# A hybrid decoder block on one core: plain fp32 for one small layer, and a new order around the output projection

## The chip, the cores and the metric

The kernel runs on one core of a Trainium2 chip. The metric is device time in microseconds (us), from the first to the last instruction of one execution and what lies around it, as the median of three runs. The engines are named as in the profile: PE is TensorE (its weight load is PEld), DVE is VectorE, ACT is ScalarE, POOL is GpSimd, SP is SyncE, which here only issues transfers.

## The reference, cut to what matters

One decoder layer on 256 tokens of width 1024: attention by two groups of heads, then a feed-forward layer that picks experts out of 16,384 (PEER). What the change touches is the compressed branch (a small two-layer network over blocks of 32 tokens), the six modulation vectors that come from the condition `c`, and the output projection.

```python
cond = jax.nn.silu(c)
mod = (cond @ ada_w[l] + ada_b[l]).reshape(c.shape[0], 6, 1, D_MODEL)
sh_a, sc_a, g_a, sh_f, sc_f, g_f = (mod[:, i] for i in range(6))
h = rmsnorm(x, norm1_g[l]) * (1 + sc_a) + sh_a
x = x + g_a * nsa_diff_mixer(h, w_in[l], w_out[l], ...)     # mixed @ w_out at its end
h = rmsnorm(x, norm2_g[l]) * (1 + sc_f) + sh_f
x = x + g_f * peer_ffn(h, peer_wq[l], peer_sub_keys[l], peer_u[l], peer_v[l])

def compress_blocks(tok, pos_enc, w1, w2, starts):          # called for keys and for values
    idx = starts[:, None] + np.arange(CMP_BLOCK)[None, :]
    blocks = tok[:, idx] + pos_enc[None, None, :, None, :].astype(tok.dtype)
    ...
    return jax.nn.gelu(flat @ w1) @ w2                      # w1: 2048 x 256
```

In the differential heads `o_d` is normed (a square root of a mean of squares) before it joins the mixed row.

## The kernel before, in words

**Stages.** Up to 64 us the input projection runs for the first 16 chunks of 128 columns (`k_load`, `k_prep`, `k_mm`, lines 211 to 242). From there to about 145 us come the attention heads, the compressed branch and the rest of the input projection, then the tail of the heads and the output projection (to 184 us), four early chunks of the expert layer's query product (L743), the second norm, and from 202 us the expert layer: 128 tiles of `peer_u` (products L89 to L91 for the name `up`), the choice of experts, and 128 tiles of `peer_v`.

**Products in three parts.** A weight tile of 128 x 1024 is loaded into one of 5 `raw` buffers by SP (`load`, L67), ACT casts it to a high part `w_hi` (L73), DVE subtracts to get `w_lo` (L74), and `mm3` (L88) multiplies high by high (L89) and the two mixed terms (L90, L91). So each such tile costs one ACT and one DVE instruction, and three products for one. In two places plain fp32 products of one pass of the code are used instead, without a split: L743 and L865, both for the expert layer's queries.

**The compressed branch.** `evac_ctok` (L308) adds the position code to the token columns in PSUM, writes the sum to a buffer and splits it into `e_sb` (high) and `cd` (low); `cmp_gen` (L380) takes 8 tiles of `cmp_w1`, 4 for keys and 4 for values, splits each, and issues 4 x 3 products of 256 columns with 30 stationary columns. Then come a Gelu (L391), two transposes (L395) and the small second layer.

**The order of the work** between 64 and 184 us is written out by hand: each word of `ORDER` advances one generator by one step, and the compiler's scheduler then places the instructions on the engines, near that order. The words: `cmp` the compressed branch; `nA`, `nB` the rest of the input projection; `ds0` to `ds3` and `do0`, `do1` the differential heads' logits and outputs; `pgt`, `ogt` and `ct` logits, outputs and the compressed part of the other heads (group g, half t); `w0` to `w3` the output projection with the first half (kh=0) of its inputs, which are the NSA heads' rows. Its second half (kh=1), fed by the differential heads, follows after `ORDER` in a loop of its own (`w_out_part(dp, 1, ...)`, L706).

**The late modulation sums.** 24 of the 40 column tiles of `ada_w` are summed late (`more_ada`, L192): SP loads 512 KB into one of 4 `adal` buffers, DVE multiplies by `cond` and sums (L151). `ada` does that at its place, `adf` only after the last marked instruction. What is left over after `ORDER` is summed there. The sums are needed for the residual (`mod` at L711) and for the second norm, so after the second half of the output projection's first tile.

**Differential heads' output** (`diff_out`, L587): transposes (L595), copies by ACT (`dpt`, L597), products with the values (L603), squares with sums by ACT (L609), a square root by ACT (L610, needs the table of square roots), reciprocal and product by DVE (L611, L612: `od`), transposes, and a split into `mixed` (L620 by ACT, L621 by DVE). kh=1 of the output projection needs `mixed` from both `do1` and `do0`.

**Second norm and queries.** After the projection PE sums squares (L704), ACT takes the root (L733), DVE the reciprocal (L734); then DVE and ACT make the normed rows (L756 to L759), and `bq`, `qe` (L764 to L766) empty the early query products' banks. The same banks hold the first `up` tiles.

Of the kernel before, what the change touches and what calls it, by code (L numbers as in the profile page):

```python
# [13 lines left out]
F32 = mybir.dt.float32  # L14
F32R = mybir.dt.float32r
# [4 lines left out]
AF = mybir.ActivationFunctionType  # L20
# [4 lines left out]
P = 128  # L25
D = 1024
# [9 lines left out]
nB cmp p01 cmp p00 cmp c0 p11 o01 o01 nB p11 adf o01 ada ada p00 c0 ada ada p00 o01 p11 p11 p00 o00  # L36
o00 adf p11 p11 p11 p10 adf p11 p10 p11 p11 o11 p10 p10 p10 o01 adf p10 ds3 o11 adf o01 p10 ds3 p10
ds3 p10 o11 p10 p10 o11 adf ds3 ds2 ds3 ds2 ds2 ds3 o10 ds2 ds2 o00 ada ada o00 o10 adf do1 o10 o10
o11 ada adf adf adf do1 ds2 adf o11 adf do0 do1 w0 do0 do0 do1 w0 w1 do1 w2 ada do0 w2 do0 w1 w3 ada
w3 ada  # L40
""".split()
KD = 8
T = 256
# [14 lines left out]
def block_kernel(ctx: ExitStack, tc: tile.TileContext, I, out):  # L58
    nc = tc.nc
    V, S, G, PE = nc.vector, nc.scalar, nc.gpsimd, nc.tensor  # L60
# [6 lines left out]
    def load(src, n=D, pool=None, name="raw", **kw):  # L67
        t = (pool or raw_pool).tile([P, D], F32, name=name, **kw)
        nc.sync.dma_start(t[:, :n], src)
        return t  # L70

    def split(src, hi, lo, eng=None):
        S.copy(hi, src)  # L73
        return (eng or V).tensor_sub(lo, src, hi.bitcast(F32))  # L74

    def split_tile(t, n=D, eng=None):
        hi = hl_pool.tile([P, D], F32R, name="w_hi")
        lo = hl_pool.tile([P, D], F32R, name="w_lo")
        split(t[:, :n], hi[:, :n], lo[:, :n], eng)
        return hi, lo  # L80

    def load_split(src, n=D, eng=None, first=False):
        if first:
            with tc.high_priority(offset=None if first is True else first):
                return split_tile(load(src, n), n, eng)
        return split_tile(load(src, n), n, eng)

    def mm3(ps, w, m, start, stop):  # L88
        PE.matmul(ps, w[0], m[0], start=start, stop=False)  # L89
        PE.matmul(ps, w[0], m[1], start=False, stop=False)  # L90
        PE.matmul(ps, w[1], m[0], start=False, stop=stop)  # L91
# [23 lines left out]
    sm = ph1.enter_context(tc.tile_pool(name="sm", bufs=4))  # L115
# [5 lines left out]
    def bank(tag):  # L121
        return (pst if tag == "tr" else psp).tile([P, 512], F32, name=tag)
# [3 lines left out]
    eps_t = one.tile([P, 1], F32, name="eps_t")  # L126
# [13 lines left out]
    w2 = cmpc[:, 32:544].rearrange("p (a b c) -> p a b c", a=2, b=2)  # L140
# [9 lines left out]
    def ada_sum(ct, w):  # L150
        return V.tensor_tensor_reduce(out=w, in0=w, in1=cond, scale=D / 2, scalar=0.0,  # L151
                               op0=ALU.mult, op1=ALU.add, accum_out=mod[:, ct:ct + 1])
# [39 lines left out]
    def more_ada(fence=False):  # L192
        ct = next(pend_ada, None)
        if ct is None:
            return
        w = wk.tile([P, D], F32, name="adal", bufs=4)
        nc.sync.dma_start(w, I["ada_w"][ct])
        if fence and mark:
            with tc.issue_after(mark[-1].ins):
                ada_sum(ct, w)  # L200
        else:
            ada_sum(ct, w)
# [73 lines left out]
    wk = wk_stack.enter_context(tc.tile_pool(name="wk", bufs=2))  # L276
# [8 lines left out]
    def projN(name, n, per, evac):  # L285
# [14 lines left out]
        for t in range(2):  # L300
# [1 line left out]
        yield  # L302


    ctok = [[wk.tile([P, 512], F32R, name=n, bufs=b).rearrange("p (o b) -> p o b", o=16)
             for n, b in (("e_sb", 8), ("cd", 2))] for kv in range(2)]

    def evac_ctok(kv):  # L308
        def f(ps):
            full = wk.tile([P, 512], F32, name="lg_sb", bufs=3).rearrange("p (o b) -> p o b", o=16)  # L310
            for g in range(2):
                src = ps[g * 64:(g + 1) * 64].rearrange("p (b o) -> p o b", o=16)
                for half in range(2):
                    pr = slice(64 * half, 64 * half + 64)
                    V.tensor_add(full[pr, :, g * 15:(g + 1) * 15], src[:, :, half:half + 15],
                                 pos[pr, kv, :, None].to_broadcast([64, 16, 15]))
            hi, lo = [x[:, :, 0:30] for x in ctok[kv]]
            return split(full[:, :, 0:30], hi, lo)
        return f


# [58 lines left out]
    def cmp_gen():  # L380
        for kv in range(2):
            hps = bank("tr")
            for l in range(4):
                hi, lo = load_split(I["cmp_w1"][kv, l], D)
                for o in range(4):
                    c = slice(o * 256, (o + 1) * 256)
                    mm3(hps[:30, 0:256], [x[:, l * 4 + o, 0:30] for x in ctok[kv]], (hi[:, c], lo[:, c]),
                        l == 0 and o == 0, l == 3 and o == 3)
                yield
            hd = wk.tile([P, T], F32, name="on", bufs=1)  # L390
            S.activation(hd[:30], hps[:30, 0:256], AF.Gelu_apprx_tanh)  # L391
            yield
            tp = bank("tr")
            for hh in range(2):
                PE.transpose(tp[:, hh * 32:hh * 32 + 30], hd[:30, hh * P:(hh + 1) * P], ident[:30, :30])  # L395
            V.tensor_copy(hidT[kv][:, :, 0:30], tp[:, 0:64].rearrange("p (a b) -> p a b", a=2)[:, :, 0:30])
            yield
            if kv == 0:
                ps = bank("tr")
                for hh in range(2):  # L400
                    PE.matmul(ps[:, 0:30], w2[:, 0, hh], hidT[0][:, hh, 0:30], start=hh == 0, stop=hh == 1)
                for x in KC:
                    S.copy(x.rearrange("p g c -> p (g c)"), pcz[0][:, 0, 0:32])
                for g in range(2):
                    pr = slice(64 * g, 64 * g + 64)
                    split(ps[pr, g * 15:g * 15 + 15], KC[0][pr, g, 0:15], KC[1][pr, g, 0:15])
                done.add("KC")
            else:
                ps = bank("tr")
                for g in range(2):  # L410
                    for hh in range(2):
                        PE.matmul(ps[0:15, g * 64:g * 64 + 64], hidT[1][:, hh, g * 15:g * 15 + 15],
                                  w2[:, 1, hh, 0:64], start=hh == 0, stop=hh == 1)
                for g in range(2):
                    for h in range(4):
                        S.copy(vbd[g][32 * h:32 * h + 15, 64 * h:64 * h + 64], ps[0:15, g * 64:g * 64 + 64])
                done.add("vbd")
            yield
# [236 lines left out]
    def item(n):  # L655
        if n[:2] == "ds":
            return diff_soft(int(n[2]))
        if n[:2] == "do":
            return diff_out(int(n[2]))
        if n == "nA":  # L660
            return projN("w_inA", 280, 3, evacA)
        if n == "nB":
            return projN("w_inB", 512, 2, evacB)
        if n == "cmp":
            return cmp_gen()
        h = int(n[1])
        if n[0] == "c":
            return nsa_c(h)
        if n[0] == "p":
            return nsa_p(h, int(n[2]))  # L670
        if n[0] == "o":
            return nsa_o(h, int(n[2]))
        if n[0] == "w":
            return w_out_part(h, 0, WO[h])
        raise ValueError(n)

    items = {}
    for n in ORDER:
        if n in ("ada", "adf"):
            more_ada(n == "adf")  # L680
        else:
            if n not in items:
                items[n] = item(n)
            next(items[n], None)
# [53 lines left out]
    for i, tag in enumerate(("o", "tr", "mm", "mm")):  # L738
        with tc.high_priority(offset=None):
            w = load(I["peer_wq"][i])  # L740
# [539 lines left out]
```

## Time and profile before

| | |
|---|---|
| time, median of 3 runs | 971.66 us (971.08 to 974.53) |
| the profiled execution | 968.78 us, of which its span 967.0 us |
| PE busy, DVE busy, ACT busy | 927.8, 765.9, 496.2 us |
| mean granted TensorE clock | 0.990 |
| data moved | 197.55 MB, 204 GB/s over the span |

The span is what the trace shows, from the first to the last instruction; the time has some 1.8 us more around it. A busy time sums an engine's instructions; since matrix products are pipelined and their ends are modelled, a stretch in which PE counts as fully busy can still be one in which it runs at half clock. The clock stands in the windows as a share of 2.4 GHz: 1.00 and 0.50 are its two levels, and values between them are stretches that hold both.

### The profile page before, as it was taken

Reading aid. Unit: us, or ns where it says so; the run is one execution under the profiler, and the core shown is the slowest. Engines: PE = TensorE matmul, PEld = TensorE weight load, DVE = VectorE, ACT = ScalarE, POOL = GpSimd, SP = SyncE. Lnnn points to the kernel's source line nnn. Section 1 sums busy time; section 2 is a strip of 40 time slices with the busy share of each in tenths; the row PEclk is TensorE's granted clock in tenths of the full one; section 3 lists DMA queues with packets and bytes.
Section 4 is the critical chain, followed back from the end, with each engine's and each line's share of the span. In section 5 each row is a group of like instructions: output and inputs, shape, how many; then the busy total and the mean of one; then the engine's idle time right before and its main releaser. Section 6 shows DMA issues by size and latency. Waiting matters only on the chain.

```text
span 967.0 us, 18674 instructions
## 1 busy us (share of the span) xinstructions
PE 927.8 (96%) x7118; PEld 681.8 (71%) x7118; DVE 765.9 (79%) x2033; ACT 496.2 (51%) x901; POOL 14.5 (2%) x27
## 2 busy tenths in 40 slices
PE   5989997999999999999999999999999998999995
PEld 3987877888888888899999998444544543554442
DVE  7978888788475799468988988799999988655664
ACT  4458874574333465554444445545444544555552
POOL 0000010000000000000000000000000000000001
PEclk9999998999999999999999999999999999999998
DMA  9978557686544356755555555655555669756631
GB/s 361 357 296 267 156 176 239 236 293 190 181 156 155 123 176 200 234 195 184 177 189 181 178 192 177 217 198 181 191 193 182 214 218 331 233 177 198 212 112 48
DMA packets 54132, 197.55 MB, mean 204 GB/s; under 512 B 6145, under 2 KB 6417, under 8 KB 53522
## 3 DMA queue, kind: packets, MB, share of 16 engines
q1 hardware_dynamic: 52706, 191.38, 59.2%
q0 software_dynamic: 608, 3.17, 1.0%
q10 hardware_dynamic: 720, 1.74, 0.5%
q8 instruction: 57, 0.93, 0.4%
q14 instruction: 41, 0.34, 0.1%
HBM read 193.11 MB, written 3.15 MB: 203 GB/s over the span
## 4 chain that ended last, share of the span: by engine, by line
PE 85%; DVE 6%; DMA 4%; ACT 3%; issue 2%; SPq 0%; DVEq 0%; ACTq 0%
PE y L1077 28%; PE up L89 11%; PE up L90 11%; PE up L91 11%; PE up L865 4%; PE gps L988 3%; DMA raw<-in_ada_w_dram 2%; PE lg L350 2%; PE mm L90 1%; PE mm L91 1%; PE mm L89 1%; PE o L524 1%; DMA raw<-in_w_inK_dram 1%; PE gps L873 1%; DVE w_hi L794 1%
## 5 line engine op out<-in xcount | busy, mean ns | idle before, releaser
L1077 PEld LDWEIGHTS <-wt 128*128 128x128 f16 x1500 | 144.0, 98 | 170.3 <-DVE wt L794 5.1
L793 ACT ACTIVATE w_lo<-raw 128x1024 f16<-128x1024 f32 x128 | 135.2, 1057 | 173.7 <-PE y L1077 84.3
L793 ACT ACTIVATE w_hi<-raw 128x1024 f16<-128x1024 f32 x128 | 135.2, 1056 | 170.2 <-PE up L91 85.8
L794 DVE SCALAR_TENSOR_TENSOR w_lo<-raw,w_lo 128x1024 f16<-128x1024 f32 x128 | 156.3, 1221 | 62.9 <-ACT w_lo L793 60.5
L794 DVE SCALAR_TENSOR_TENSOR w_hi<-raw,w_hi 128x1024 f16<-128x1024 f32 x128 | 156.1, 1219 | 54.9 <-ACT w_hi L793 54.6
L1077 PE MATMUL y<-w_hi,wt 128*128 128x512 f16 x756 | 174.0, 379 | 2.0 <-DVE wt L794 2.0
L1077 PE MATMUL y<-w_lo,wt 128*128 128x512 f16 x744 | 171.0, 379 | 0.5 <-DVE wt L794 0.4
L89 PE MATMUL up<-h,w_hi 128*128 128x256 f16 x512 | 139.6, 273 | 2.1 <-ACT bq L765 2.1
L91 PE MATMUL up<-h,w_hi 128*128 128x256 f16 x512 | 139.6, 273 | 0.0
L90 PE MATMUL up<-h,w_hi 128*128 128x256 f16 x512 | 139.6, 273 | 0.0
L89 PE MATMUL up<-h,w_lo 128*128 128x256 f16 x504 | 137.4, 273 | 0.0
L91 PE MATMUL up<-h,w_lo 128*128 128x256 f16 x504 | 137.4, 273 | 0.0
L90 PE MATMUL up<-h,w_lo 128*128 128x256 f16 x504 | 137.4, 273 | 0.0
L794 DVE SCALAR_TENSOR_TENSOR wt<-st,wt 128x256 f16<-128x256 f32 x128 | 53.6, 419 | 4.7 <-ACT wt L793 4.7
L90 PEld LDWEIGHTS <-w_hi 128*128 128x128 f16 x512 | 50.1, 98 | 8.2 <-issue 2.3
L793 ACT ACTIVATE wt<-st 128x256 f16<-128x256 f32 x128 | 51.3, 401 | 7.6 <-PE y L1077 5.6
L90 PEld LDWEIGHTS <-w_lo 128*128 128x128 f16 x512 | 50.1, 98 | 6.1
L91 PEld LDWEIGHTS <-w_hi 128*128 128x128 f16 x512 | 50.1, 98 | 5.8
L91 PEld LDWEIGHTS <-w_lo 128*128 128x128 f16 x512 | 50.0, 98 | 5.8
L89 PEld LDWEIGHTS <-w_lo 128*128 128x128 f16 x512 | 50.1, 98 | 5.7
L89 PEld LDWEIGHTS <-w_hi 128*128 128x128 f16 x512 | 50.2, 98 | 5.5
L972 DVE TENSOR_TENSOR B<-iota,kT 128x576 f16<-128x576 f16 (+1 forms) x64 | 27.1, 424 | 28.9 <-PE gps L988 28.8
(366 smaller groups left out, 1489.2 us busy)
## 6 DMA issues: line engine op xcount, KB each, us to landing
raw<-in_peer_u_dram SPq DMA_DIRECT2D x128, 512.0 KB, 3.5
raw<-in_peer_v_dram SPq DMA_DIRECT2D x128, 512.0 KB, 3.8
adal<-in_ada_w_dram SPq DMA_DIRECT2D x24, 512.0 KB, 4.5
adaw<-in_ada_w_dram SPq DMA_DIRECT2D x16, 512.0 KB, 5.5
raw<-in_w_inK_dram SPq DMA_DIRECT2D x16, 512.0 KB, 7.4
wraw<-in_peer_wq_dram SPq DMA_DIRECT2D x12, 512.0 KB, 4.3
raw<-in_cmp_w_dram SPq DMA_DIRECT2D x8, 512.0 KB, 4.4
raw<-in_w_out_dram SPq DMA_DIRECT2D x8, 512.0 KB, 4.4
```

Of the source, the lines that this page charges most:

```text
L89: PE.matmul(ps, w[0], m[0], start=start, stop=False)
L90: PE.matmul(ps, w[0], m[1], start=False, stop=False)
L91: PE.matmul(ps, w[1], m[0], start=False, stop=stop)
L350: PE.matmul(out, q[x][pr, ts], rhs, start=i == 0, stop=i == 2)
L524: PE.matmul(o[:, h * 64:(h + 1) * 64], pt[:, h * P:(h + 1) * P], vst[sb][:, b, g], start=False, stop=bi == len(blocks) - 1 and h == 3)
L793: S.activation(hi, src, AF.Copy, scale=scale, **kw)
L794: V.scalar_tensor_tensor(lo, src, scale, hi, ALU.mult, ALU.subtract, accum_out=chk[:, i:i + 1])
L865: PE.matmul(ps, w[:, k * P:(k + 1) * P], h2[:, k], start=k == 0, stop=k == KD - 1)
L873: PE.matmul(sps[:, t], qs[p][:, t * P:(t + 1) * P], sk[:, p], start=True, stop=True)
L972: V.tensor_tensor(pairs(x), io, kT[:, i, t0:t0 + NT, None, :].to_broadcast(four), ALU.is_equal)
L988: PE.matmul(ps[:, q, 0:n], A[:, q], Bg[i][:, q], start=i == 0, stop=i == 1)
L1077: PE.matmul(yps[t][n], w[:, ts], m[:, ns], start=j == 0 and first, stop=j == NJ - 1 and last)
```

## The change

It has three parts. First, the compressed branch's first layer takes the unsplit token columns and the unsplit weight tile: 16 plain fp32 products for each of keys and values in the place of 48, with no ACT cast, no DVE subtraction, and the `raw` buffer held until the products are done. Second, the last lines of `ORDER` are rewritten: the modulation sums that stood between `o00`, `do1` and `o11` stand among and after `w0` to `w3`. Third, a word `sqrt` issues a square root of one column, ahead of `do0`.

```diff
-o11 ada adf adf adf do1 ds2 adf o11 adf do0 do1 w0 do0 do0 do1 w0 w1 do1 w2 ada do0 w2 do0 w1 w3 ada
-w3 ada
+o11 ada adf do1 ds2 o11 sqrt do0 do1 w0 do0 do0 do1 w0 adf w1 do1 adf w2 adf do0 w2 do0 w1 adf w3 adf ada
+w3 ada ada
...
-    ctok = [[wk.tile([P, 512], F32R, name=n, bufs=b).rearrange("p (o b) -> p o b", o=16)
-             for n, b in (("e_sb", 8), ("cd", 2))] for kv in range(2)]
+    ctok = [wk.tile([P, 512], F32, name="e_sb", bufs=8).rearrange("p (o b) -> p o b", o=16) for kv in range(2)]
...
-                    V.tensor_add(full[pr, :, g * 15:(g + 1) * 15], src[:, :, half:half + 15],
+                    r = V.tensor_add(ctok[kv][pr, :, g * 15:(g + 1) * 15], src[:, :, half:half + 15],
                                  pos[pr, kv, :, None].to_broadcast([64, 16, 15]))
-            hi, lo = [x[:, :, 0:30] for x in ctok[kv]]
-            return split(full[:, :, 0:30], hi, lo)
+            return r
...
-                hi, lo = load_split(I["cmp_w1"][kv, l], D)
+                w = load(I["cmp_w1"][kv, l])
                 for o in range(4):
-                    c = slice(o * 256, (o + 1) * 256)
-                    mm3(hps[:30, 0:256], [x[:, l * 4 + o, 0:30] for x in ctok[kv]], (hi[:, c], lo[:, c]),
-                        l == 0 and o == 0, l == 3 and o == 3)
+                    PE.matmul(hps[:30, 0:256], ctok[kv][:, l * 4 + o, 0:30], w[:, o * 256:(o + 1) * 256],
+                              start=l == 0 and o == 0, stop=l == 3 and o == 3)
...
+        elif n == "sqrt":
+            S.activation(sm.tile([P, 1], F32, name="root"), eps_t, AF.Sqrt)
```

**In the built order, DVE ahead of the second half of the output projection.** Before, from the reciprocal of `do0`'s norm (`rd`) on; `adal` is a modulation sum, `w_lo` a weight tile's split, `mixed` the split of `do0`'s rows:

```order
L611 RECIPROCAL rd<-rd 128x4
L151 ISA adal,mod<-adal,cond 128x1024
L151 ISA mod 128x1
L612 TENSOR_TENSOR od<-o,rd 128x512
L155 TENSOR_TENSOR mod<-mod,rows 128x24
L74 TENSOR_TENSOR w_lo<-raw,w_hi 128x1024
L692 SCALAR_TENSOR_TENSOR gs_2037<-mod,rows 128x8
L74 TENSOR_TENSOR w_lo<-raw,w_hi 128x1024
L621 SCALAR_TENSOR_TENSOR mixed_70<-tr,subs,mixed_69 128x4x128
```

With the change, from the same reciprocal on:

```order
L607 RECIPROCAL rd<-rd 128x4
L74 TENSOR_TENSOR w_lo<-raw,w_hi 128x1024
L608 TENSOR_TENSOR od<-o,rd 128x512
L151 ISA adal,mod<-adal,cond 128x1024
L151 ISA mod 128x1
L151 ISA adal,mod<-adal,cond 128x1024
L151 ISA mod 128x1
L617 SCALAR_TENSOR_TENSOR mixed_70<-tr,subs,mixed_69 128x4x128
L151 ISA adal,mod<-adal,cond 128x1024
L151 ISA mod 128x1
L151 ISA adal,mod<-adal,cond 128x1024
L151 ISA mod 128x1
```

Here the `w_lo` is that of `w3`'s first half. The first split for kh=1 stands right behind the last of these sums; before, two splits for kh=1 stood ahead of `do0`'s `mixed`, with one sum between the reciprocal and them.

**ACT at the start of the program.** Before, `th` being the condition's tanh:

```order
L136 DMA rows<-in_rows_dram 128x65
L251 ACT_TABLE_LOAD
L251 ACTIVATE th<-lg 128x512 x2
L254 ACTIVATE sq_111<-xT 128x1024 x2
L403 CAST KC_749<-pcz_757 128x32
```

With the change:

```order
L136 DMA rows<-in_rows_dram 128x65
L678 ACT_TABLE_LOAD
L678 ACTIVATE root<-eps_t 128x1
L251 ACT_TABLE_LOAD
L251 ACTIVATE th<-lg 128x512 x2
```

The new square root (L678) needs only the constant `eps_t`, and stands at the head of the program, a table load with it, ahead of the first tanh.

**ACT ahead of the expert layer**, where the normed rows `h` are made between the first casts of `peer_u` tiles (`w_hi` and `w_lo` at L793 are two buffers for casts), and `bq` empties the early query products' banks. Before:

```order
L793 ACTIVATE w_hi<-raw 128x1024
L766 ACTIVATE qe<-qe,bq 128x256
L765 COPY bq<-tr 128x1
L765 COPY bq<-mm 128x1
L793 ACTIVATE w_lo<-raw 128x1024
```

With the change:

```order
L791 ACTIVATE w_hi<-raw 128x1024
L756 ACTIVATE h_2152,big<-bias,shs 128x256
L791 ACTIVATE w_lo<-raw 128x1024
L764 ACTIVATE qe<-qe,bq 128x256 x2
L763 COPY bq<-mm 128x1 x2
```

The `w_lo` cast of one more `peer_u` tile and a second `qe` now stand ahead of the copy `bq<-mm`, and that copy of `tr` further up.

## Rows read from the trace of the kernel before

**Rows 1.** The page: busy time of each engine (part 1) and the chain by engine (part 4).

```profile
PE 927.8 (96%) x7118; PEld 681.8 (71%) x7118; DVE 765.9 (79%) x2033; ACT 496.2 (51%) x901; POOL 14.5 (2%) x27
...
PE 85%; DVE 6%; DMA 4%; ACT 3%; issue 2%; SPq 0%; DVEq 0%; ACTq 0%
```

**Rows 2.** What TensorE (PE) waited for, 64 to 90 us: us in total, times, longest.

```profile
PE mm L89 <- DVE q L336: 3.0, 1, 3.0
PE tr L395 <- ACT on L391: 1.4, 1, 1.4
PE tr L90 <- DVE w_lo L74: 0.3, 1, 0.3
```

**Rows 3.** What PE waited for, 190 to 960 us.

```profile
PE y L1077 <- DVE wt L794: 2.4, 4, 1.2
PE up L89 <- ACT bq L765: 2.1, 1, 2.1
```

**Rows 4.** TensorE's timeline from 64 us: start, us, engine, line, operation, out<-in, shape, count.

```profile
72.62 0.28 PE L89 MATMUL tr<-w_hi,e_sb 128*30 128x256 f32 x1
...
73.68 0.28 PE L89 MATMUL tr<-w_hi,e_sb 128*30 128x256 f32 x1
```

**Rows 5.** The same view from 236 us: plain fp32 products of the query layer.

```profile
238.00 7.07 PE L865 MATMUL up<-h,wraw 128*128 128x256 f32 x32
```

**Rows 6.** The same view where the output projection ends and the expert layer begins.

```profile
183.64 0.28 PE L91 MATMUL o<-mixed,w_lo 128*128 128x256 f32 x1
...
202.16 0.27 PE L89 MATMUL up<-h,w_hi 128*128 128x256 f16 x1 [2.07 <-ACT bq L765]
```

**Rows 7.** What TensorE waited for, 145 to 172 us.

```profile
PE mm L91 <- DVE w_lo L74: 2.7, 1, 2.7
```

**Rows 8.** VectorE's (DVE) timeline, 149 to 170 us.

```profile
155.63 1.23 DVE L151 CUSTOM_DVE_ANT_0 adal<-adal,cond 128x1024 f32<-128x1024 f32 x1 [0.63 <-DMA adal<-in_ada_w_dram]
...
156.78 1.22 DVE L74 TENSOR_TENSOR w_lo<-raw,w_hi 128x1024 fp32r<-128x1024 f32 x1
...
159.12 0.68 DVE L612 TENSOR_TENSOR od<-o,rd 128x512 f32<-128x512 f32 x1
...
165.72 0.75 DVE L621 SCALAR_TENSOR_TENSOR mixed<-tr,subs,mixed 128x512 fp32r<-128x512 f32 x1 [0.47 <-ACT mixed L620]
```

**Rows 9.** ScalarE's (ACT) timeline: the first table load, and that of the differential heads' norm.

```profile
1.15 1.28 ACT L251 ACT_TABLE_LOAD   x1 [1.15 <-PEq L1272]
4.54 0.60 ACT L251 ACTIVATE th<-lg 128x512 f32<-128x512 f32 x1 [2.11 <-PE lg L250]
...
153.05 1.28 ACT L610 ACT_TABLE_LOAD   x1
154.34 0.30 ACT L610 ACTIVATE rd<-rd,eps_t 128x4 f32<-128x4 f32 x1
```

**Rows 10.** Stretches of 2 us: busy time of PE, PEld, DVE, ACT, POOL, then TensorE's clock.

```profile
68.00:70.00 2.00, 1.77 (x8) 1.44 (x7) 1.94 (x5) 1.01 (x3) 0.00 (x0) 0.50 1.02 391
70.00:72.00 2.00, 1.92 (x10) 1.81 (x11) 1.52 (x5) 0.73 (x3) 0.00 (x0) 0.66 1.06 338
158.00:160.00 2.00, 1.95 (x9) 1.95 (x10) 2.00 (x5) 0.00 (x0) 0.00 (x0) 0.50 0.73 223
...
162.00:164.00 2.00, 2.00 (x13) 2.00 (x12) 0.07 (x2) 1.05 (x1) 0.00 (x0) 0.62 0.78 305
...
200.00:202.00 2.00, 0.09 (x1) 0.00 (x0) 2.00 (x8) 2.00 (x7) 0.19 (x1) 1.00 1.01 358
```

**Rows 11.** ScalarE's timeline ahead of the expert layer, 189 to 203 us.

```profile
198.24 1.04 ACT L793 ACTIVATE w_lo<-raw 128x1024 f16<-128x1024 f32 x1
...
201.51 0.50 ACT L766 ACTIVATE qe<-qe,bq 128x256 f32<-128x256 f32 x1
...
201.95 0.15 ACT L765 COPY bq<-mm 128x1 f32<-128x1 f32 x1
```

**Rows 12.** The page, part 6: DMA loads, KB each, median us from issue to landing.

```profile
adal<-in_ada_w_dram SPq DMA_DIRECT2D x24, 512.0 KB, 4.5
```

More of the change, by code (lines that the diff above doesn't have):

```diff
@@ L302, in projN @@
         yield
-    ctok = [[wk.tile([P, 512], F32R, name=n, bufs=b).rearrange("p (o b) -> p o b", o=16)
-             for n, b in (("e_sb", 8), ("cd", 2))] for kv in range(2)]
+    ctok = [wk.tile([P, 512], F32, name="e_sb", bufs=8).rearrange("p (o b) -> p o b", o=16) for kv in range(2)]
     def evac_ctok(kv):
         def f(ps):
-            full = wk.tile([P, 512], F32, name="lg_sb", bufs=3).rearrange("p (o b) -> p o b", o=16)
             for g in range(2):
```

## The prediction

> **What bounds the kernel now.** I read the page first: PE is busy 96% of the span and carries 85% of the chain that ended last [rows 1]. So a change counts only where PE waits, where PE itself gets more or less to do, or where PE runs at half clock. From 190 us to the end PE waits only 4.5 us in all, 2.1 us of it before its first `up` product [rows 3]; what is won or lost before then passes through to the end. So I read PE's waits between 64 and 190 us, and the other engines only at those places. There are four. At 64 us PE waits 3.0 us for a query split, at 84 us 1.4 us for the Gelu, and twice 0.3 us for a weight split [rows 2]. At 155 us it waits 2.7 us for the weight split `w_lo` [rows 7], because VectorE stands in modulation sums: the row at 155.63 even waits 0.63 us for its own load, and the split follows at 156.78 [rows 8]. At 200 us PE waits 2.07 us for `bq` on ScalarE [rows 6]. The windows show what such waits do afterwards: behind the wait at 64 us the clock is 0.50 and 0.66, behind that at 155 us it is 0.50 to 0.62 until 164 us, but during the 2.07 us wait at 200 us it stays 1.00 [rows 10]. A stretch at half clock loses 2 x (0.50 + 0.34) = 1.7 us in the first case, and 1.0 + 1.0 + 0.76 = 2.8 us in the second (the stretch 160 to 162 reads as 158 to 160 does).
>
> **The change, part by part.**
>
> *Plain fp32 in the compressed branch.* Removed: 96 products; three triples take 73.68 - 72.62 = 1.06 us, so 0.353 us for a triple [rows 4]. Added: 32 plain products of the same 256 columns. None exists with 30 stationary columns; the nearest row has 32 records, two to a product, in 7.07 us, of which 0.16 us is the last one's overhang: 6.91 / 16 = 0.432 us [rows 5]. So PE gets 32 x 0.079 = +2.5 us. The Trainium skill, in "FP8 and Floating Point Precision", section "TensorE Precision Notes", counts four passes of the array for true fp32; at three passes for a triple that would be 0.470 us each by the triple's row, and +3.8 us. The row of the same kind decides, so +2.5 stays. ACT loses eight casts and DVE eight subtractions of about 1.2 us each (one like them in [rows 8]), all hidden behind PE except at the waits: the wait at 64 us shrinks, since the branch's own split stood ahead of the query's (an estimate of 0.4 us: 480 columns at 1.22 us for 1024 are 0.57, not all of it on the path); the 1.4 us for the Gelu goes, since other products now stand there; both 0.3 us waits go. Together +2.5 - 0.4 - 1.4 - 0.6 = **+0.1 us**. Bounds: -2.4 if the added work falls wholly into waits, +2.5 if no wait shrinks.
>
> *The sums moved.* The two splits for `w0` and `w1` now come long before 150 us, and the one for `w2` right behind the last head's `mixed` split, so PE's wait at 155 us goes. What is late next is the second half, kh=1: the same eight late sums still precede its first split. I walk VectorE's queue from the root `rd`, which ends at 154.34 + 0.30 = 154.64 [rows 9]; a 1.22 us operation takes 1.15 us from start to start (155.63 to 156.78), an `od` 0.60, a `mixed` of `do1` or `do0` 0.67 [rows 8], each less the 0.08 by which the next one overlaps it. Reciprocal 154.73, `od` 155.3, two sums 157.6, `mixed` 158.3, one sum 159.4, reciprocal 159.5, `w_lo` of `w3` 160.7, `od` 161.3, two sums 163.6, `mixed` 164.3, two sums 166.6, first split for kh=1 **167.7**. The loads of these sums keep up: each is issued when the sum four places ahead is done, the last at 159.4, and lands 4.5 us later [rows 12] at 163.9. PE has `w3`'s 24 products behind 160.7, so is through at about 163.9, and then waits 3.8 us. kh=1 is 96 products at a third of a triple, 0.118 us, so 11.3 us: the projection ends at 179.0 instead of 183.64 + 0.12 = 183.76 [rows 6], **-4.8 us** at full clock. If the 3.8 us wait lowers the clock, 1.7 to 2.8 us of that is lost.
>
> *The tail.* Ahead of the expert layer ACT is the path: PE's first `up` product waits for `bq<-mm`, which in the new order stands behind one more cast (0.96 us to the next start, of the 1.04 us in [rows 11]) and one more `qe` (0.40): **+1.4 us**. On DVE a `peer_u` split now precedes the first normed row, which fills a pause that ACT had, and costs nothing beyond that. PE's wait becomes 2.07 + 1.4 + 0.44 (one early query product moved ahead of the sum of squares, into a pause) = 3.9 us, longer than the 3.0 us that had a clock of 0.50 behind it: 0 or 1.7 us more. Bounds 0 (if the banks are free otherwise) and +3.1.
>
> *The root's table.* It doesn't do what it says: the scheduler puts the new root at the head of the program, and the load for the norm stays where it was, so its 1.28 us stays on the chain of the walk above. At the head, ACT's two loads and the root end near 1.15 + 2 x 1.28 + 0.3 = 4.0 us, before the 4.54 us at which the tanh can start [rows 9]: 0.
>
> *The sum.* Two waits, of 3.8 and 3.9 us, may lower the clock. In the rows 2.07 us did not and 3.0 us did, and what decides for waits a little longer than that they don't show, so I take one of the two as slowed: 0.1 - 4.8 + 1.4 + 1.7 = **-1.6 us**. The profiled execution took 968.78 us, 2.9 us under the median of 971.66; I take the change off both: 967.2 for such an execution, **970.1 us** for the median. With neither wait slowed it is 968.4, with both 971.8; that is this case's own range.
>
> **The rivals.**
>
> *Relief everywhere (faster).* Waits between 64 and 145 us go while the added work falls into pauses (-2.4), no clock falls (-4.8), and the banks are free early enough (0): -7.2, 964.5 us. For it: VectorE is busy at 79% and in the stretch before the wait far more, so lifting 16 long operations off ACT and DVE may help in places where I see none. Against it: PE has few waits there to give back.
>
> *Only moved.* The walk starts later, because `do1`'s products now queue on PE behind products of `w0` and `w1`, and the root with them. Each us there is a us at the end; with 4.8 us lost, what remains is +0.1 + 3.1 = +3.2: 974.9 us. For it: the eight sums remain, 8 x 1.15 = 9.2 us of VectorE.
>
> *Late loads (slower).* The compressed branch's weights now hold their `raw` buffer until PE is through with them, not until the split. SP issues in order, so a load behind waits with all that follow. It decides where a buffer comes free less than 4.5 us (a landing [rows 12]) plus a cast and a split of about 1.1 us each before PE needs the next tile, 6.7 us in all. Two such loads with nothing ahead cost 2 x 4.5 = 9.0 us: -1.6 + 9.0 = +7.4, 979.1 us. Against it: five buffers, and PE runs these products close together.
>
> *A dearer table switch.* In the trace the root at 154.34 starts as its load ends, 153.05 + 1.28 [rows 9]. If a switch took twice that at the head, the tanh would come at 1.15 + 4 x 1.28 + 0.3 = 6.6 instead of 4.54: +2.0, 972.1 us. The Trainium skill, "ScalarE: Activation LUTs", section "What ACT_TABLE_LOAD costs", gives 1.28 us for the load and 1.38 us for a drain with each switch; the row agrees with the load and shows no drain.
>
> **How the numbers follow.** A measurement of this kernel can tell about 0.5%, 4.86 us, from no change: faster is below 966.8, slower above 976.5. Chances: the forecast 0.47, relief 0.25, only moved 0.15, late loads 0.10, dearer switch 0.03. The forecast, the third and the last lie within 0.5%, 0.65; faster 0.25; slower 0.10. The range takes in the forecast's own, the case "only moved" with a us to spare, and goes below to where half of the relief case lies: **965.0 to 976.0**; outside are late loads and part of relief.
>
> **What would show it.** Right: no PE wait for `w_lo` near 155 us, and a new one of 3 to 4 us that ends near 168 us with VectorE in two sums before it; a wait of 3.5 to 4 us for `bq` before the first `up`; compressed products at 0.43 us each; a table load still ahead of `rd`. Wrong: a wait for `bq` no longer than before (the tail's term falls), an end of the projection later than 182 us (the walk falls), a wait for a load between 64 and 140 us, or compressed products far from 0.43 us.

## The result and the profile after

The changed kernel took **976.56 us** in the median of 20 runs (971.59 to 986.32), the kernel before beside it 971.72 us (20 runs, 969.52 to 974.53): a ratio of 1.0056 [1.0031, 1.0082]. A second series, run c1 below, gave 974.41 us in 12 runs (970.34 to 985.4) and 1.0042 [1.0019, 1.0064]. The ratios, here and below, leave out executions more than 1.5% above the fastest of the same kernel, the one of 986.32 us among them. So the change costs about half a per cent where 0.16% less was forecast, and 976.56 lies just above the range. It also spreads its executions over 15 us, where the kernel before has 5.

Two executions of the changed kernel are shown. That of c1 (973.8 us, span 972.0) lies near the median and is the one that the ledger uses. The first one (986.32 us, span 984.5) shows how far the same loss can go.

First the page of c1: engines' busy time and TensorE's clock in 40 slices.

```profile
PE 935.0 (96%) x7086; PEld 681.9 (70%) x7086; DVE 757.2 (78%) x2023; ACT 489.7 (50%) x893; POOL 14.7 (2%) x27
...
PEclk9999989989999999999999999999999999999998
```

PE's share is the 96% of before [rows 1], with 7 us more of busy time; DVE has lost 9 us of work and ACT 6.5, and it did not help. A busy share can't show the reason, since half clock counts as busy; in the row of the clock the sixth and the ninth slice (of 24.3 us each) read 8, and where the clock falls inside them the windows below show.

What TensorE waited for in c1, the four longest waits (us in total, times, longest).

```profile
PE up L89 <- ACT bq L763: 4.7, 1, 4.7
PE mm L89 <- DVE q L333: 2.7, 1, 2.7
PE mm L91 <- DVE w_lo L74: 2.4, 1, 2.4
PE mm L89 <- DVE dq L333: 1.3, 1, 1.3
```

Of [rows 2, 7]: the 3.0 us for the query split became 2.7, the Gelu's 1.4 us is gone, and a new wait of 1.3 us for `dq` stands near it. The wait for `w_lo` is the new one, for the second half; the old one at 155 us is gone. The wait for `bq` [rows 3] grew from 2.1 to 4.7 us.

The windows of 2 us of c1: busy time of PE, PEld, DVE, ACT, POOL, then TensorE's clock.

```profile
130.00:132.00 2.00, 2.00 (x16) 1.81 (x14) 2.00 (x8) 2.00 (x8) 1.07 (x1) 0.88 0.12 41
132.00:134.00 2.00, 2.00 (x8) 1.53 (x7) 0.86 (x2) 0.46 (x3) 0.00 (x0) 0.50 0.01 2
...
138.00:140.00 2.00, 2.00 (x15) 1.75 (x15) 0.77 (x3) 1.10 (x5) 0.00 (x0) 0.92 0.17 61
...
172.00:174.00 2.00, 1.18 (x5) 1.18 (x6) 2.00 (x5) 0.20 (x1) 0.00 (x0) 0.62 0.22 37
174.00:176.00 2.00, 2.00 (x12) 2.00 (x11) 1.29 (x3) 0.00 (x0) 0.00 (x0) 0.53 0.89 283
...
204.00:206.00 2.00, 0.51 (x3) 0.38 (x3) 1.31 (x4) 2.00 (x7) 0.19 (x1) 0.50 0.96 324
206.00:208.00 2.00, 2.00 (x11) 1.34 (x10) 0.00 (x0) 0.38 (x1) 0.00 (x0) 0.50 1.00 410
208.00:210.00 2.00, 2.00 (x11) 1.40 (x10) 0.00 (x0) 0.00 (x0) 0.00 (x0) 0.50 1.00 420
```

The rows of 172 and 204 us and those behind them are half clock behind the two waits: 0.62 and 0.53 from 172 us, 0.50 from 204 to 210. The first three rows are what the prediction has nothing about: from about 131.5 to 138.3 us the clock is 0.50 while PE is counted busy for 2.00 of 2 us, and in this stretch PE waits for nothing. The two windows left out between 132 and 138 read 0.50 too, and the kernel before has 1.00 in all five; one of them stands at c2 below. Windows of the same kind from the other execution, 986.32 us:

```profile
134.00:136.00 2.00, 2.00 (x7) 1.54 (x8) 0.00 (x0) 0.00 (x0) 0.00 (x0) 0.50 0.53 166
...
164.00:166.00 2.00, 2.00 (x16) 1.80 (x15) 1.70 (x5) 0.37 (x1) 0.00 (x0) 0.87 0.38 74
```

Here half clock begins at about 134 us and lasts until 165: 31 us in which half of the work that full clock would do is lost, some 15 us. That is most of the 12.5 us by which this execution is longer than c1's, which lost 3.4 us here.

The rest of the marks that the prediction named. TensorE's timeline of c1 (start, us, engine, line, operation, out<-in, shape, count): one group of the plain products, the projection's last product, the first `up`.

```profile
79.95 5.37 PE L383 MATMUL tr<-raw,e_sb 128*30 128x256 f32 x24
...
184.44 0.28 PE L91 MATMUL o<-mixed,w_lo 128*128 128x256 f32 x1
...
205.49 0.37 PE L89 MATMUL up<-h,w_hi 128*128 128x256 f16 x1 [4.67 <-ACT bq L763]
```

VectorE's timeline of c1, from the reciprocal of the late root to the first split of the second half, with the split for `w3` (164.60) and the last sum (170.41) between.

```profile
159.60 0.18 DVE L607 RECIPROCAL rd<-rd 128x4 f32<-128x4 f32 x1 [1.70 <-ACT rd L606]
...
164.60 1.19 DVE L74 TENSOR_TENSOR w_lo<-raw,w_hi 128x1024 fp32r<-128x1024 f32 x1
...
170.41 1.22 DVE L151 CUSTOM_DVE_ANT_0 adal<-adal,cond 128x1024 f32<-128x1024 f32 x1
...
171.55 1.22 DVE L74 TENSOR_TENSOR w_lo<-raw,w_hi 128x1024 fp32r<-128x1024 f32 x1
```

ScalarE's timeline of c1: the head of the program, and the norm of the differential heads.

```profile
1.16 1.28 ACT L678 ACT_TABLE_LOAD   x1 [1.16 <-PEq L1270]
2.45 0.20 ACT L678 ACTIVATE root<-eps_t 128x1 f32<-128x1 f32 x1
2.67 1.28 ACT L251 ACT_TABLE_LOAD   x1
4.35 0.60 ACT L251 ACTIVATE th<-lg 128x512 f32<-128x512 f32 x1 [0.40 <-PE lg L250]
...
157.98 1.28 ACT L606 ACT_TABLE_LOAD   x1
159.27 0.30 ACT L606 ACTIVATE rd<-rd,eps_t 128x4 f32<-128x4 f32 x1
```

The new root (L678) stands at the head, and the load ahead of `rd` (L606) stayed. At the head two loads and the root end at 3.95 us and the tanh starts at 4.35, earlier than the 4.54 of [rows 9]. The root at 2.45 and `rd` at 159.27 start as their loads end.

ScalarE's timeline of c1 ahead of the expert layer.

```profile
203.54 1.06 ACT L791 ACTIVATE w_lo<-raw 128x1024 f16<-128x1024 f32 x1 [0.69 <-DMA raw<-in_peer_u_dram]
...
204.51 0.89 ACT L764 ACTIVATE qe<-qe,bq 128x256 f32<-128x256 f32 x2
205.30 0.20 ACT L763 COPY bq<-mm 128x1 f32<-128x1 f32 x2
```

The cast ahead of `qe` waited 0.69 us for its own load, which [rows 11] has not.

### The profile page after: what moved, and what is told of

It reads as the page before. It is cut to its first block, busy times and chain, and to the rows that moved or that the text cites. A ratio compares the mean times of both kernels' runs of the same rounds, so it can differ in the third digit from the quotient of the medians.

```text
span 984.5 us, 18574 instructions
## 1 busy us (share of the span) xinstructions
PE 947.2 (96%) x7086; PEld 692.3 (70%) x7086; DVE 757.8 (77%) x2023; ACT 490.3 (50%) x893; POOL 14.7 (1%) x27
## 4 chain that ended last, share of the span: by engine, by line
PE 86%; DVE 6%; DMA 4%; ACT 2%; issue 2%; DVEq 0%; ACTq 0%
PE y L1075 28%; PE up L89 11%; PE up L90 11%; PE up L91 11%; PE up L863 4%; PE gps L986 3%; DMA raw<-in_ada_w_dram 3%; PE lg L347 2%; PE o L520 2%; PE tr L383 2%; PE mm L89 1%; PE mm L90 1%; PE mm L91 1%; DMA raw<-in_peer_u_dram 1%; PE tr L513 1%
```

## The experiments

The change has three parts: plain fp32 products, later sums, the root. Two theories stood against each other: that the plain products, by freeing ACT and DVE, let the scheduler rearrange PE's work so that the clock falls at 131 us; or that the moved sums cost more, through the two longer waits, than they give back. The first four runs share one set of runs of the kernel before (971.57 us).

**The change once more (c1).** No edit.

> The changed kernel once more, for more runs and for a trace of a quick run. Its 20 runs lie in two groups: ten from 971.6 to 974.5 us at a mean clock of 0.984 to 0.988, ten from 978.7 to 986.3 at 0.972 to 0.981. Both theories expect the two groups again, and in a trace of the lower group no half clock between 120 and 165 us or only a few us of it, with the wait for bq before the first up product near 4.8 us in either.

Measured: 974.41 us, 1.0042 [1.0019, 1.0064]; its profile stands above. The half clock at 131 us came again, so it belongs to the kernel, and so do the two groups: nine runs up to 975.1 us and three from 979.2.

**Plain fp32 alone (c2).** The changed kernel with the last lines of the old order.

```diff
-o11 ada adf do1 ds2 o11 sqrt do0 do1 w0 do0 do0 do1 w0 adf w1 do1 adf w2 adf do0 w2 do0 w1 adf w3 adf ada
-w3 ada ada
+o11 ada adf adf adf do1 ds2 adf o11 adf do0 do1 w0 do0 do0 do1 w0 w1 do1 w2 ada do0 w2 do0 w1 w3 ada
+w3 ada
```

> The first part alone: plain fp32 in the compressed branch, the order of the work as before. Theory A (the plain products, and what they shift behind them, make the clock fall between 120 and 165 us): two groups of runs as in the whole change, median 974 to 980 us, with half clock in the trace in some runs. Theory B (the new order does it): one narrow group within 2 us of the kernel before, 970 to 974 us, and no half clock between 100 and 150 us.

Measured: 973.76 us, 0.9996 [0.9966, 1.0026], from 964.98 to 981.37. The twelve runs follow the mean clock: three of 965.0 to 967.4 us at 0.992 to 0.993, six of 976.2 to 981.4 at 0.975 to 0.980. TensorE's timeline and windows of its profile (970.45 us):

```profile
119.17 0.48 PE L91 MATMUL mm<-w_hi,h_lo 128*128 128x512 f32 x1
119.48 1.00 PE L520 MATMUL o<-vst,pt 128*128 128x64 f32 x8
...
124.48 0.39 PE L347 MATMUL lg<-KH,q 64*128 64x512 f32 x1
...
132.02 1.46 PE L520 MATMUL o<-vst,pt 128*128 128x64 f32 x6
```

```profile
132.00:134.00 2.00, 2.00 (x9) 1.86 (x9) 1.51 (x4) 1.10 (x6) 0.00 (x0) 0.53 0.00 0
134.00:136.00 2.00, 2.00 (x7) 1.21 (x6) 0.00 (x0) 0.00 (x0) 0.00 (x0) 0.50 0.70 258
```

Call a product wide that has 512 columns on all 128 rows. The last of them (`mm<-w_hi,h_lo`, of the rest of the input projection) is at 119.17 us. Nine logits products of 512 columns on 64 rows follow, the last at 124.48, and behind these come only products of 64 to 256 columns. At 119.48 us eight products of 64 columns take 1.00 us; at 132.02 six take 1.46, about twice as long for each. No wait lies between. (The clock also reads 0.71, 0.50 and 0.93 from 162 to 168 us.) But the kernel before has its last wide product at nearly the same place, and its clock stays at 1.00. Its timeline of TensorE, and its window of 132 us:

```profile
118.95 0.39 PE L91 MATMUL mm<-w_hi,h_lo 128*128 128x512 f32 x1
```

```profile
132.00:134.00 2.00, 2.00 (x17) 1.75 (x16) 2.00 (x8) 1.00 (x4) 0.00 (x0) 1.00 0.31 88
```

So the fall at 131 us comes with the plain products and not with the moved sums, but where the wide products end does not tell the two kernels apart. The three quickest executions of c2 lie 4 to 7 us below the median of the kernel before.

One place where it helps is seen in the list of TensorE's waits of c2, 145 to 172 us. The longest is:

```profile
PE o L599 <- ACT dpt L593: 1.2, 1, 1.2
```

The 2.7 us for `w_lo` at 155 us [rows 7] are gone, although the sums stand where they stood. c5 and c11 below, with the old order of the sums too, have no such wait either, c11 even with VectorE's old load. So plain fp32 alone takes away the wait that the sums were moved for; by what way is not traced.

**The new order alone (c3).** The kernel before with the new last lines and the root.

> The second and third part alone: the new order and the root, the compressed branch split as before. Theory A: one narrow group, 968 to 973 us (the walk of VectorE gains up to 4.8 us at the projection, the tail gives 1.4 to 4.8 us back), no half clock between 100 and 150 us. Theory B: two groups, with runs above 977 us.

Measured: 972.8 us (972.12 to 974.83), 1.0021 [1.001, 1.0031], so 1 to 3 us slower, where the prediction's terms for these parts come to -4.8 + 1.4 + 1.7 = -1.7. The clock is 1.00 from 76 to 170 us, and the spread is gone. VectorE's and TensorE's timelines of its profile:

```profile
152.57 3.48 DVE L74 TENSOR_TENSOR w_lo<-raw,w_hi 128x1024 fp32r<-128x1024 f32 x3
155.98 0.17 DVE L611 RECIPROCAL rd<-rd 128x4 f32<-128x4 f32 x1
...
168.64 1.22 DVE L74 TENSOR_TENSOR w_lo<-raw,w_hi 128x1024 fp32r<-128x1024 f32 x1
...
182.03 0.28 PE L91 MATMUL o<-mixed,w_lo 128*128 128x256 f32 x1
...
202.64 0.37 PE L89 MATMUL up<-h,w_hi 128*128 128x256 f16 x1 [4.61 <-ACT bq L767]
```

Three weight splits stand in a row ahead of `rd`'s reciprocal, and the first split of the second half starts at 168.64. PE ends the projection at 182.03 instead of 183.64 [rows 6], 1.6 us earlier where the walk gave 4.8, and loses 2.1 us again by the first `up` (20.61 us later, before 18.52). Half clock stands behind both waits (170 to 174 and 200 to 208 us).

**Without the root (c4).** The change with `sqrt` taken out of the order.

```diff
-o11 ada adf do1 ds2 o11 sqrt do0 do1 w0 do0 do0 do1 w0 adf w1 do1 adf w2 adf do0 w2 do0 w1 adf w3 adf ada
+o11 ada adf do1 ds2 o11 do0 do1 w0 do0 do0 do1 w0 adf w1 do1 adf w2 adf do0 w2 do0 w1 adf w3 adf ada
```

> The change without the early root. Its table load stands at the head of the program, hidden: both theories expect the same as the whole change, two groups, the lower near 973 us. A rival (the early load costs time) expects about 2 us less in both groups.

Measured: 978.58 us (973.64 to 985.76), 1.0081 [1.005, 1.0111]. The intervals of c1 and c4 overlap, and both kernels spread over the same 12 to 15 us, so an effect of the root can't be told from none. Its profile has the fall too: 0.63, 0.50, 0.50 and 0.66 from 132 to 140 us.

The next three share another set of runs of the kernel before (971.65 us).

**Plain fp32 with the wide products spread (c5).** c2 with two steps of `nB` (wide products of the rest of the input projection) moved in among the small ones.

```diff
-nB cmp p01 cmp p00 cmp c0 p11 o01 o01 nB p11 adf o01 ada ada p00 c0 ada ada p00 o01 p11 p11 p00 o00
-o00 adf p11 p11 p11 p10 adf p11 p10 p11 p11 o11 p10 p10 p10 o01 adf p10 ds3 o11 adf o01 p10 ds3 p10
+cmp p01 cmp p00 cmp c0 p11 o01 o01 p11 adf o01 ada ada p00 c0 ada ada p00 o01 p11 p11 p00 o00
+o00 nB adf p11 p11 p11 p10 adf p11 p10 p11 p11 o11 p10 p10 p10 o01 adf nB p10 ds3 o11 adf o01 p10 ds3 p10
```

> Plain fp32 in the compressed branch, the old order, but the last two steps of nB (24 products of 512 columns) moved later, among the small products of the stretch from 119 to 133 us. Theory A1 (the clock falls because PE, though counted as busy, does only small products there: 64 columns, transposes, logits on 64 rows): clock 1.00 from 100 to 150 us, one narrow group of runs near the best of the plain fp32 kernel, 964 to 968 us. Theory A2 (the plain fp32 products themselves make it fall, wherever the rest lies): half clock between 125 and 140 us again, runs spread from 965 to 981 us.

Measured: **965.41 us** (six runs, 965.24 to 967.02), 0.9946 [0.9926, 0.9966]. Its timeline of TensorE and its windows:

```profile
123.34 0.50 PE L90 MATMUL mm<-w_lo,h_hi 128*128 128x512 f32 x1
...
132.13 0.48 PE L89 MATMUL mm<-w_hi,h_hi 128*128 128x512 f32 x1
```

```profile
132.00:134.00 2.00, 2.00 (x14) 1.53 (x12) 1.27 (x6) 1.47 (x5) 0.00 (x0) 1.00 0.24 66
```

Wide products stand at 123 and at 130 to 132 us, and the clock stays 1.00 there, and from 76 us on as far as 288 us. All six runs have the time of c2's fastest, 6 us below the kernel before, with the sums where they were. The move took the fall away. Since the kernel before has no wide products there either and keeps its clock, it does not show that their absence is what lowers it.

**The kernel before with the wide products early (c6).** The reverse: `nB` taken out of the later place.

```diff
-p01 p01 p00 ds0 cmp p01 p00 cmp cmp p11 ds1 ds1 ds1 p01 cmp c1 cmp p00 c1 ds1 c0 p00 p00 p00 c1 p00
-nB cmp p01 cmp p00 cmp c0 p11 o01 o01 nB p11 adf o01 ada ada p00 c0 ada ada p00 o01 p11 p11 p00 o00
+p01 p01 p00 ds0 cmp p01 p00 cmp cmp p11 ds1 ds1 ds1 p01 cmp c1 cmp p00 c1 ds1 c0 p00 nB p00 p00 c1 p00
+nB cmp p01 cmp p00 cmp c0 p11 o01 o01 p11 adf o01 ada ada p00 c0 ada ada p00 o01 p11 p11 p00 o00
```

> The kernel before, with the compressed branch split in three, but the last steps of nB moved earlier, so that the stretch after about 112 us holds only small products, as with plain fp32. Theory A1: half clock for some us between 120 and 145 us in some runs, times from 971 up to 985 us. Theory A2: no half clock there, 970 to 974 us.

Measured: 972.77 us, 1.0011 [0.9998, 1.0024]. Its last wide product starts at 116.96 us, and yet the clock is 1.00 from 78 to 158. A long stretch without wide products is therefore not enough to lower the clock, as the kernel before shows already; the simple form of that theory falls.

**The new order with `bq` first (c7).** c3 with the copy that `up` waits for put ahead of what else ScalarE has there.

```diff
-        S.copy(bq[:, i:i + 1], ps[:, T:T + 1])
+        with tc.high_priority(offset=None):
+            S.copy(bq[:, i:i + 1], ps[:, T:T + 1])
```

> The new order without plain fp32, as in the run of the order alone (972.8 us), but the copies bq get priority, so that one cast of a peer_u tile less stands ahead of the first bq<-mm on ACT. If the tail's term is right: the wait before the first up product falls from 4.6 us to about 3, with less or no half clock behind it, 969.5 to 972 us. Rival (something else, such as the normed rows or the weights' loads, holds the first up product): the wait stays at 4 to 5 us under another name, 972 to 974 us.

Measured: 969.42 us (968.71 to 971.73), 0.998 [0.9968, 0.9992], so 3.4 us less than c3. TensorE's wait before the first `up`:

```profile
PE up L89 <- ACT bq L768: 2.0, 1, 2.0
```

It was 4.6 in c3, and about 3 was expected; the first `up` starts at 200.96 instead of 202.64. The clock behind it is still low, 0.53 and 0.61 from 202 to 206, although a wait of 2.07 us in the kernel before left it at 1.00. So the added wait was ScalarE's order, as the prediction said, and a bound on a wait's length does not tell alone what the clock does.

The next three: 971.79 us for the kernel before.

**The change mended (c8).** The changed kernel with c5's `nB` and c7's `bq`.

> The whole change with both costs mended: nB's last steps moved among the small products, and bq first. The lower group of the change lies near 973 us. If its two costs add up: about 3 us less, since the half clock from 131 to 138 us goes, and about 3.4 us less at the tail, as the run of the order with bq first showed: 966 to 968 us, one narrow group, and still a wait of 2 to 3 us for the first split of kh=1. Rival (the costs are not independent, one wait takes the place of the other): 969 to 973 us.

Measured: 968.7 us (965.98 to 974.45), 0.9973 [0.9959, 0.9986], between the two expectations and in no narrow group. Two of the twelve runs are at 974.2 and 974.5 with a mean clock of 0.982. One of them has the profile; its windows, and two wide products where the clock falls:

```profile
110.00:112.00 2.00, 2.00 (x10) 1.28 (x9) 1.02 (x7) 1.26 (x6) 0.00 (x0) 0.89 0.75 264
112.00:114.00 2.00, 2.00 (x12) 1.48 (x11) 0.68 (x6) 0.35 (x2) 0.00 (x0) 0.50 0.08 31
...
124.00:126.00 2.00, 2.00 (x11) 1.23 (x10) 1.89 (x7) 0.89 (x2) 0.00 (x0) 0.69 0.00 0
...
132.00:134.00 2.00, 2.00 (x17) 1.73 (x16) 1.20 (x7) 0.72 (x5) 0.00 (x0) 1.00 0.17 31
```

```profile
111.19 0.40 PE L89 MATMUL mm<-w_hi,h_hi 128*128 128x512 f32 x1
...
111.71 0.63 PE L91 MATMUL mm<-w_hi,h_lo 128*128 128x512 f32 x1
```

132 us is at 1.00 now, but half clock stands at 111 to 125 us. It begins in a row of wide products, so these do not keep the clock up by themselves. c5 has the same order up to here and keeps 1.00 in its profile.

**The same with six sums early (c9, again as c12).** c8 with six `ada` steps moved up, so that they no longer stand ahead of the late splits.

```diff
-o00 nB adf p11 p11 p11 p10 adf p11 p10 p11 p11 o11 p10 p10 p10 o01 adf nB p10 ds3 o11 adf o01 p10 ds3 p10
-ds3 p10 o11 p10 p10 o11 adf ds3 ds2 ds3 ds2 ds2 ds3 o10 ds2 ds2 o00 ada ada o00 o10 adf do1 o10 o10
+o00 nB adf p11 p11 p11 p10 adf p11 p10 ada p11 p11 o11 p10 ada p10 p10 o01 adf nB p10 ds3 o11 ada adf o01 p10 ds3 ada p10
+ds3 p10 o11 ada p10 p10 o11 adf ds3 ada ds2 ds3 ds2 ds2 ds3 o10 ds2 ds2 o00 ada ada o00 o10 adf do1 o10 o10
```

> As before this one, but six of the late sums moved up among the logits, where VectorE has pauses with plain fp32. If the eight sums ahead of kh=1 are what VectorE's queue costs there, the wait for its first split goes, with the half clock behind it: 2 to 4 us less than the mended change, 962 to 965 us. Rival (the loads or the differential heads' norm hold kh=1): the same as the mended change within 1 us.

> The mended change with six sums moved up, once more, since it had only four runs: 960 to 965 us in most, up to 968 where the clock falls, and below the kernel before by 0.7 to 1.2%. If the four runs were lucky: 966 to 970 us.

Measured: 962.62 us (four runs), 0.9898 [0.9884, 0.9913], and again on another chip **962.38 us** (five runs, 961.85 to 964.6), 0.9903 [0.9889, 0.9917] beside 972.16 for the kernel before. The two longest waits of TensorE in c12 between 64 and 215 us:

```profile
PE mm L89 <- DVE q L333: 2.7, 1, 2.7
PE tr L702 <- DVE sqd L720: 1.1, 1, 1.1
```

Both the wait for `w_lo` and that for `bq` are gone, and the first `up` starts at 195.35 us instead of 202.16 [rows 6]. In this profile the clock is 1.00 from 76 us on as far as 288 us. The profile of c9, its longest run (967.69 us), still has half clock at 112 to 115 and 148 to 156 us.

**The early sums without the new last lines (c10).** c5 with `bq` first and the six sums early.

> Plain fp32, nB spread, bq first and six sums moved up, but with the old order of the last lines (no new order of the sums, no root). If the new order adds nothing once the sums are up early: within 1 us of the run with the new order, 962 to 965 us. Rival: the new order still gives a gain of its own, 1 us or more.

Measured: 966.67 us (five runs), 0.9949 [0.9936, 0.9962]. By its interval it is no better than c5, and behind c9 by 4 us, as the rival expected. That may be the new last lines, or in part the clock: its runs have a mean clock of 0.987 to 0.992, those of c12 0.992 or 0.993. The two aren't separated.

**Plain products with the splits left in (c11).** c2, and each of the eight weight tiles is still cast and subtracted as before; the two results are used by nothing.

```diff
                 w = load(I["cmp_w1"][kv, l])
+                split_tile(w)
```

> Plain fp32 alone, as in the run of that part, but the casts and subtractions of the eight weight tiles are done all the same and not used, so that ACT and DVE are as loaded as before. If the plain products on PE are enough to make the clock fall: half clock between 120 and 145 us again in some runs, and times spread from about 967 up to 983 us. If it is the shift of the rest (with ACT and DVE relieved the scheduler runs the wide products of nB in one block and leaves only small ones behind): no half clock between 100 and 150 us, and one narrow group, 970 to 975 us.

Measured: 970.05 us (968.0 to 971.92), 0.9974 [0.9965, 0.9984]. PE's products are c2's, but ACT and DVE carry the old load: the clock is 1.00 from 78 to 204 us and the spread is 4 us instead of 16. So the fp32 products alone do not lower the clock; it falls where ACT and DVE have been freed with them. By what way that reaches PE is not shown: the last wide product starts at 120.8 us here, at 119.2 in c2 and at 119.0 in the kernel before.

## Why the prediction was wrong

**The ledger, by the marks.** The profile of c1 is 5.0 us longer than that of before (spans 972.0 and 967.0), which was forecast to be 1.6 shorter. By the medians of that series it is 2.8, since the profiled execution of before was a short one. Up to the projection's end the change lost 0.8 us (184.44 against 183.64), from there to the first `up` 2.5 (21.05 against 18.52 us), and behind that 2.25 at half clock (one window of 2 us twice, and half a us of a third); together 5.6, of which later stretches give 0.6 back.

**The step that failed: plain fp32 "+0.1", with the added work hidden and full clock taken for granted.** The price of a product was right: in the row of 79.95 us twelve products take 5.37 - 0.16 = 5.21 us, 0.434 each, forecast 0.432. The Trainium skill's four passes ("FP8 and Floating Point Precision", section "TensorE Precision Notes"), taken as 4/3 of a triple, give an estimate of 0.470: measured is 1.23 of a triple. What was left out is that with the casts and subtractions gone the clock falls where PE waits for nothing. From 130 to 140 us that loses 0.24 + 3 x 1.00 + 0.16 = 3.4 us in c1, and from 134 to 165 us some 15 in the longest run. Plain fp32 alone (c2) has the fall, the new order alone (c3) has none in this stretch, plain fp32 with the old load on ACT and DVE (c11) has none, and with wide products put into the stretch (c5) none. No rival named this, so no part of the range stood for it. The Trainium skill ("TensorE: Matmul & The Clock Gate", section "HAM oscillation — how this bites in real kernels") ties the fall to gaps in which PE waits for data; the rows at 155 us of before agree, those at 131 us don't, for no wait is there.

The same term was wrong in what it gives. Where the clock held (c5), plain fp32 is worth 6.2 us by the medians and 3.5 by the spans, 2.9 of these by the projection's end (180.78 against 183.64), and not 0.1 us lost. It takes away the wait at 155 us, which the prediction had put down to the moved sums. So c5 comes near the 964.5 us of the rival "relief everywhere", by a wait that this rival did not name.

**The sums moved, -4.8: the walk's length was right, its start was not.** From the start of `rd`'s reciprocal to the end of the first split VectorE took 159.60 to 172.77, 13.2 us; forecast were 13.1. But the walk began 5 us later than it had been written for, and PE with it: 3.4 us of that are the half clock at 131 us, and the rest, some 1.5 us, is a later root, as the rival "only moved" had it; what delays the root is not traced. PE's wait became 2.4 us instead of 3.8, and the projection ends later than 182 us, the prediction's own sign that the walk falls. Without those 3.4 us at half clock the projection's end would stand 2.6 us earlier than before; forecast were 4.8 less 1.7 for a clock that falls behind this wait, plus 0.1, so 3.0. In c3 the scheduler put three splits ahead of the root's reciprocal, which the walk, in the built order of the whole change, hadn't got, and 1.6 us were left.

**The tail, +1.4: right in place, too small.** It cost 2.5 us. The wait is 4.67 us, forecast were 3.9. The 0.44 us by which PE was to come to it earlier did not show: it comes 16.38 us after the start of the projection's last product (205.49 - 4.67 - 184.44), before 16.45 (202.16 - 2.07 - 183.64). Of the 1.1 us beyond the forecast 0.69 are the cast's wait for its load; the other 0.4 isn't traced. c7 shows the cause to be ScalarE's order.

**One of two waits slowed, +1.7: both were.** 172 to 176 us lost 0.76 + 0.94 = 1.7, 205.5 to 210 lost 2.25. The prediction's rows gave no ground for one alone: waits of 2.7 and 3.0 us [rows 2, 7] had both had half clock behind them [rows 10], and both waits that it forecast were longer.

**The root, 0: right.** It was hoisted, the load for `rd` stayed, and c4 shows no effect that can be told from its spread. Of the rivals, "late loads" and the dearer table switch did not occur (no wait for a load between 64 and 140 us; the tanh is no later).

So the 6.6 us between forecast and profile are 3.4 of a clock that no term stood for, 2.25 of the second slowed wait, 1.1 of the tail and 0.4 of the walk, less the 0.6.

**What stays open** is what makes the clock fall at full count of busy time. A stretch of small products alone did not do it in c6 or in the kernel before; in c8 the clock fell among wide ones; the same kernel has it for 7 us in one run and for 31 in another. Shown is only which arrangements had it and which had not, and that freeing ACT and DVE is a part of it (c2 against c11). What a median execution of the kernel before loses, and where, is not on record, since its profile is a short one.

## What to carry to other kernels

Taking work off engines that are not the bottleneck is no neutral step: here it brought half clock in a stretch without waits, and the same edit took away a wait that had been put down to something else. Spreading wide products among small ones took that away in all six runs of c5, but two of twelve runs of c8 still had it, so it is worth a try and no rule. Read the clock in the windows at every stretch and in several executions, since half clock is counted as busy and stands in no list of waits; a kernel whose runs spread more than those of the one before is a reason to look there. Work that is moved late still has to be done ahead of what follows: here the wait for the late splits went only when six of the sums were moved up, in c9.

## What was not expected of the hardware

TensorE's clock fell from 1.00 to 0.50 with PE counted 2.00 of 2 us busy and no wait just ahead of it, and stayed there for 7 us (c1) or 31 us (the 986.32 us execution). It did so behind small products (c1, c2) and in a row of wide ones (c8). And a wait of the same length had both outcomes: behind 2.07 us in the kernel before the clock stayed 1.00 [rows 6, 10], and in c5 too, while behind 2.0 us in c7 it was 0.53 and behind 2.06 us in c11 0.50.
